# The first FFN's weights: split once, stored to DRAM, loaded in the second run

## The chip, the cores and the metric

The kernel runs on one core of a Trainium2 chip. The metric is the device time of one execution in microseconds; the time before is the median of three executions. The profile is of one further execution.

## The reference, cut to what matters

One layer of an encoder is applied with the same weights to two batches, a prompt of 1024 tokens and a sample of 256, each of width 1024. All is in fp32.

```
x <- LN1(alpha*x + 0.5*SwiGLU_1(x))
x <- LN2(alpha*x + W_out[RMS(S5(x)) ; RMS(Hyena(x))])
x <- LN3(alpha*x + 0.5*SwiGLU_2(x))

SwiGLU(x) = (silu(x @ w_gate) * (x @ w_up)) @ w_down     # w_gate, w_up (1024, 2816), w_down (2816, 1024)
```

The change touches the first line alone, `SwiGLU_1`. The second line has a state-space part (S5), whose matrices are made from small parameters, and long convolutions (Hyena), whose filters are made and transformed by the kernel.

## The kernel before, in words

TensorE reads its operands in a shorter fp32 format (`F32R`). To keep fp32's precision each operand is split in two parts: `hi`, its value rounded to that format, and `lo`, what the rounding left. A product is then three matmuls: hi x hi, hi x lo and lo x hi. The helper `split` (L171, L172) makes the parts: ScalarE copies the source into `hi`, VectorE subtracts `hi` from the source into `lo`.

The hidden width of 2816 is 22 tiles of 128 (`NFT`), called tiles of f. The first FFN runs twice over all its weights, since not all tokens fit in SBUF at once. `fa` (L1635) has four tiles of 128 tokens, two of the sample and two of the prompt, 512 tokens in all; `fb` (L1634) has the other six tiles of the prompt, 768 tokens, in chunks of 512 and 256. Both go through the function `ffn` (L254).

In `ffn`, a weight number i stands for one half of a tile of f: i = 2 ft is gate, i = 2 ft + 1 is up. `weights(i)` (L273) loads raw fp32 columns on SP's queue (L281) into one of two raw buffers (128 columns at a time in `fa`, 256 in `fb`) and splits 128 of them into one of two buffers `wgu`, each (128, 2, 8, 128): part, slice of the model width, column. `gate_up(ft)` (L287) calls `weights(i)` and, one ahead, `weights(i + 1)`, runs the matmuls of gate and of up (L298; per weight 24 matmuls for each chunk of tokens), and forms h = 0.5 * silu(gate) * up (L306, L307), which is split too. Down goes in groups of tiles of f: `size` is 2 by default, so nine groups of two and a last one of four. `wdown(ft)` (L316) splits a raw tile of w_down that `load_down` (L311, L314) loaded on SP's queue; `fa` has one raw buffer for these and `fb` two, and the next load is issued behind the split that frees the buffer. `down(grp, ...)` (L324) sums 3 matmuls for each tile of f of the group in one PSUM bank for each tile of tokens and half of the width (L331), and VectorE adds the bank into x (L336 for the first group, L338 for the others). Before a group's `down`, the gate and up of the next group's first tile are issued. In the last group each tile of tokens gets its layer norm and is stored to DRAM (L1601).

The work is woven: `weave` (L1644) interleaves the steps of `fa` with those of the filters (`filter_spectra`; its matmuls are on L695 to L774), and L1645 those of `fb` with the preparation of S5 (`s5_prep`, `s5_mats`: small matmuls on L611 to L628, many small VectorE operations, stores of matrices on L637 and of tables). The order of issue gives each instruction its priority, and a list scheduler, which goes by its own estimates, fixes from it the order of each engine's instructions. On the chip each engine works in that order; semaphores for every dependence are put in by the framework. DMAs of `nc.sync` are issued by SP, those of `nc.scalar` by ScalarE, those of `nc.gpsimd` by POOL. Before the change POOL issues no DMA of the program; it has the small `pow` of the layer norms (L230).

SBUF is cut in 25 pieces, which buffers take and give back. In the last group of `fb` the function `to_mix` (L1621) reloads two tiles of x1 (L1583), which `fa` had stored, and transposes them on TensorE (L221) ahead of the next stage, the in-projection (`mix_in`, L857).

## Time and profile before

| | |
|---|---|
| median of three executions | 2579.18 us (2578.24 to 2588.45) |
| the profiled execution | 2584.32 us, of which the span of the program's instructions is 2582.5 us |
| TensorE matmuls busy | 2523.1 us, 98% of the span |
| TensorE weight loads (PEld, beside the matmuls) | 2112.1 us, 82% |
| VectorE (DVE) busy | 1810.0 us, 70% |
| ScalarE (ACT) busy | 812.3 us, 31% |
| GpSimd (POOL) busy | 74.7 us, 3% |
| moved by DMA | 326.44 MB |

Busy time of TensorE is the union of its matmuls' spans, which overlap; how fast they follow each other has to be read from runs of many. `fa` and the filters take about the first 500 us, `fb` with the preparation of S5 goes on to about 1125 us. In the windows, "DMA share" is the mean busy share of the core's 16 DMA engines, and PEclk the granted share of TensorE's full clock.

### The profile page before, as it was taken

Reading aid. Unit: us, or ns where it says so; the run is one execution under the profiler, and the core shown is the slowest. Engines: PE = TensorE matmul, PEld = TensorE weight load, DVE = VectorE, ACT = ScalarE, POOL = GpSimd, SP = SyncE. Lnnn points to the kernel's source line nnn. Section 1 sums busy time; section 2 is a strip of 40 time slices with the busy share of each in tenths; the row PEclk is TensorE's granted clock in tenths of the full one; section 3 lists DMA queues with packets and bytes.
Section 4 is the critical chain, followed back from the end, with each engine's and each line's share of the span. In section 5 each row is a group of like instructions: output and inputs, shape, how many; then the busy total and the mean of one; then the engine's idle time right before and its main releaser. Section 6 shows DMA issues by size and latency. Waiting matters only on the chain.

```text
span 2582.5 us, 32676 instructions
## 1 busy us (share of the span) xinstructions
PE 2523.1 (98%) x12833; PEld 2112.1 (82%) x12833; DVE 1810.0 (70%) x3016; ACT 812.3 (31%) x1218; POOL 74.7 (3%) x58
## 2 busy tenths in 40 slices
PE   8999999999999999999999999999989999999998
PEld 6767887888888888788888878898768888888887
DVE  6777777568944666557896888788886556556437
ACT  5443344321322222223444313333332222223200
POOL 0000000000000000000000000000230000000001
PEclk9999999999999999999999999999999999999999
DMA  6332333533632333355566754564432223245311
GB/s 198 117 88 83 106 102 98 171 103 110 166 86 75 109 100 104 87 156 146 170 179 180 237 189 145 168 189 151 141 114 90 89 74 98 74 143 191 124 40 65
DMA packets 329073, 326.44 MB, mean 126 GB/s; under 512 B 41068, under 2 KB 285445, under 8 KB 328150
## 3 DMA queue, kind: packets, MB, share of 16 engines
q1 hardware_dynamic: 293366, 305.99, 37.5%
q10 hardware_dynamic: 35552, 18.36, 2.7%
q8 instruction: 101, 1.65, 0.3%
q14 instruction: 54, 0.44, 0.1%
HBM read 249.57 MB, written 74.46 MB: 125 GB/s over the span
## 4 chain that ended last, share of the span: by engine, by line
PE 82%; DVE 12%; DMA 3%; issue 2%; POOL 1%; ACT 1%; SPq 0%; DVEq 0%; ACTq 0%; POOLq 0%
PE banks L298 26%; PE banks L1367 16%; PE banks L331 12%; PE banks L1510 8%; PE banks L857 4%; PE banks L1238 3%; DVE s L927 3%; PE banks L774 3%; PE banks L1060 2%; DVE s L172 2%; PE banks L1201 1%; DVE s L245 1%; PE banks L1113 1%; DVE s L975 1%; DMA s<-in_ffn_w_gate_dram 1%
## 5 line engine op out<-in xcount | busy, mean ns | idle before, releaser
L298 PE MATMUL banks<-s,s 128*128 128x512 f32 (+1 forms) x4224 | 792.8, 342 | 3.3 <-ACT s L171 2.5
L298 PEld LDWEIGHTS banks<-s,s 128*128 128x128 f32 x4224 | 650.4, 190 | 99.6 <-issue 10.7
L171 ACT ACTIVATE s<-s 128x1024 fp32r<-128x1024 f32 (+3 forms) x467 | 437.8, 955 | 860.7 <-PE banks L298 239.0
L172 DVE TENSOR_TENSOR s<-s,s 128x1024 fp32r<-128x1024 f32 (+3 forms) x467 | 505.1, 1096 | 193.2 <-ACT s L171 191.0
L1367 PE MATMUL banks<-s,s 128*128 128x512 f32 x1848 | 423.4, 391 | 4.3 <-DVE s L172 3.4
L1367 PEld LDWEIGHTS banks<-s,s 128*128 128x128 f32 x1848 | 347.5, 188 | 78.7 <-DVE s L172 4.9
L331 PE MATMUL banks<-s,s 128*128 128x512 f32 x1584 | 393.0, 396 | 2.0 <-DVE s L172 1.0
L331 PEld LDWEIGHTS banks<-s,s 128*128 128x128 f32 x1584 | 291.2, 189 | 64.2 <-issue 2.1
L857 PE MATMUL banks<-s,s 128*128 128x512 f32 (+1 forms) x1152 | 238.1, 361 | 0.0
L1510 PE MATMUL banks<-s,s 128*128 128x512 f32 x704 | 216.8, 389 | 0.2 <-DVE s L172 0.2
L857 PEld LDWEIGHTS banks<-s,s 128*128 128x128 f32 x1152 | 188.3, 190 | 28.1 <-DVE s L172 0.4
L338 DVE TENSOR_TENSOR s<-banks,s 128x512 f32<-128x512 f32 x204 | 139.1, 688 | 49.1 <-PE banks L331 48.0
L1510 PEld LDWEIGHTS banks<-s,s 128*128 128x128 f32 x704 | 132.1, 188 | 28.1 <-DVE s L172 0.7
L1383 DVE TENSOR_TENSOR s<-banks,s 128x512 f32<-128x512 f32 x110 | 75.9, 690 | 106.5 <-PE banks L1367 105.7
L1510 PE MATMUL banks<-s 128*128 128x512 f32 x352 | 136.9, 389 | 0.0
L1238 PE MATMUL banks<-s,s 128*128 128x512 f32 x480 | 125.2, 409 | 3.2 <-ACT s L171 1.6
L1516 DVE TENSOR_TENSOR s<-banks,s 128x512 f32<-128x512 f32 x80 | 55.0, 690 | 97.1 <-PE banks L1510 97.1
L230 POOL TENSOR_TENSOR cst<-cst 128x1 f32<-128x1 f32 (+2 forms) x38 | 49.9, 1313 | 2496.0 <-DVE cst L229 2496.0
L1238 PEld LDWEIGHTS banks<-s,s 128*128 128x128 f32 x480 | 90.1, 192 | 23.1 <-ACT s L171 2.0
L307 DVE SCALAR_TENSOR_TENSOR s<-banks,s 128x512 f32<-128x512 f32 (+1 forms) x88 | 47.6, 554 | 84.3 <-PE banks L298 83.4
L543 DVE TENSOR_TENSOR s<-s,cst 128x288 f32<-128x288 f32 (+1 forms) x128 | 53.5, 438 | 53.5 <-PE banks L623 26.9
L676 DVE TENSOR_TENSOR s<-banks,s 128x512 f32<-128x512 f32 (+2 forms) x112 | 59.2, 552 | 44.4 <-ACT s L793 20.4
(210 smaller groups left out, 2347.8 us busy)
## 6 DMA issues: line engine op xcount, KB each, us to landing
s<-in_ffn_w_down_dram SPq DMA_DIRECT2D x88, 512.0 KB
s<-in_ffn_w_gate_dram SPq DMA_DIRECT2D x66, 512.0 KB
s<-in_ffn_w_up_dram SPq DMA_DIRECT2D x66, 512.0 KB
s<-in_ffn_w_gate_dram SPq DMA_DIRECT2D x11, 1024.0 KB
s<-in_ffn_w_up_dram SPq DMA_DIRECT2D x11, 1024.0 KB
scr_h<-s SPq DMA_DIRECT2D x22, 512.0 KB
s<-scr_h SPq DMA_DIRECT2D x22, 512.0 KB
scr_tab<-s ACTq DMA_DIRECT2D x64, 160.0 KB
```

The source lines that it names most:

```text
L171: K.nc.scalar.activation(out=hi, in_=src, func=AF.Copy)
L172: K.nc.vector.tensor_tensor(out=lo, in0=src, in1=hi.bitcast(F32), op=ALU.subtract)
L298: nc.tensor.matmul(pss[-1][c], lhsT=w[:, wv, d], rhs=xT.parts[k][c].at(d), start=(d == 0 and wv == 0 and k == 0), stop=(d == 7 and wv == 1))
L331: nc.tensor.matmul(ps, lhsT=h[s // 4][:, a, s % 4 * 128:(s % 4 + 1) * 128], rhs=w[:, b, dh * 512:(dh + 1) * 512], start=(n == 0), stop=(n ...
L338: nc.vector.tensor_tensor(out=xv, in0=ps, in1=xv, op=ALU.add)
L774: nc.tensor.matmul(ps, lhsT=F[kt][a].v[:, s, i], rhs=b.v[:, s], start=(n == 0), stop=(n == 3 * NT // R - 1))
L857: nc.tensor.matmul(p, lhsT=w[:, wv, d], rhs=xT[nm].parts[k][c].at(d), start=(d == 0 and wv == 0 and k == 0), stop=(d == 7 and wv == 1))
L927: TT = lambda o, a, b, op: V.tensor_tensor(out=o, in0=a, in1=b, op=op)
L1238: nc.tensor.matmul(ps, lhsT=y[s // per][a].v[:, k, ts], rhs=W[k].v[:, b, dh * 512:dh * 512 + 512], start=(k == 0 and a == 0 and b == 0), s ...
L1367: self.K.nc.tensor.matmul(ps, lhsT=w[i][:, d], rhs=x[k][:, d], start=first and m == 0, stop=m == len(todo) - 1, skip_group_check=True)
L1383: TT = lambda o, a, b: V.tensor_tensor(out=o, in0=a, in1=b, op=ALU.add)
L1510: nc.tensor.matmul(ps, lhsT=p[a].v[:, 1, o:o + 128], rhs=p[b].v[:, 0, dh * 512:dh * 512 + 512], start=m == 0, stop=m == len(todo) - 1)
```

## The change

`fa` gets a setting `keep`: after each split of a weight, SP stores both its parts to DRAM, as (128, 2, 8, 128) for each of 44 gate/up weights and as (128, 2, 1024) for each of 22 down weights, 1 MB (8 KB a partition) each. `fb` gets `parts`: it has no raw buffers and no splits of weights, and POOL loads the stored parts straight into the buffers that the matmuls read. `fb` also gets three `wgu` buffers in place of two, and `size` 3: six groups of three tiles of f and the last one of four, with three buffers for down's parts and four for h.

```diff
@@ -259,7 +259,8 @@
     unit, size = cfg.get("unit", 1), cfg.get("size", 2)
     chunks = chunks_of(T)
     fw = cfg.get("raw", 256)
-    raw = K.ring(2, 8, fw)
+    parts, keep = cfg.get("parts"), cfg.get("keep")
+    raw = None if parts else K.ring(2, 8, fw)
     wgu = K.ring(cfg.get("wgu", 2), 2, 8, 128, dt=F32R)
     bg = Banks(K, cfg["bg"])
     bd = Banks(K, cfg["bd"])
@@ -274,6 +275,10 @@
 
         ft, up = divmod(i, 2)
         if ft >= NFT or i in ready:
+            return
+        if parts:
+            ready[i] = w = wgu.get()
+            nc.gpsimd.dma_start(out=w, in_=parts[0][i])
             return
         o = ft * 128 % fw
         if o == 0:
@@ -283,6 +288,8 @@
         ready[i] = w = wgu.get()
         with K.tc.high_priority(offset=cfg.get("ahead", 0)):
             split(K, rawgu[up][:, :, o:o + 128], w[:, 0], w[:, 1])
+        if keep:
+            nc.sync.dma_start(out=keep[0][i], in_=w.bitcast(F32))
 
     def gate_up(ft):
         pss = []
@@ -297,7 +304,7 @@
             for d, wv, c, k in todo:
                 nc.tensor.matmul(pss[-1][c], lhsT=w[:, wv, d], rhs=xT.parts[k][c].at(d),
                                  start=(d == 0 and wv == 0 and k == 0), stop=(d == 7 and wv == 1))
-        if ft == NFT - 1:
+        if ft == NFT - 1 and raw:
             raw.free()
         hv = [h.get() for h in hr] if ft < NFT - 4 + size + 1 else [extra(2, n) for _, n in chunks]
         with K.tc.high_priority(offset=cfg.get("hp", 0)):
@@ -309,15 +316,20 @@
         return hv
 
     def load_down(ft):
-        if ft < NFT:
+        if ft < NFT and not parts:
             rawdn[ft] = rawd.get()
             nc.sync.dma_start(out=rawdn[ft], in_=wd[ft * 128:(ft + 1) * 128, :])
 
     def wdown(ft):
+        w = wdn.get() if ft < NFT - 4 + size else extra(2, D)
+        if parts:
+            nc.gpsimd.dma_start(out=w, in_=parts[1][ft])
+            return w
         r = rawdn.pop(ft)
-        w = wdn.get() if ft < NFT - 4 + size else extra(2, D)
         with K.tc.high_priority(offset=cfg.get("ahead", 0)):
             split(K, r, w[:, 0], w[:, 1])
+        if keep:
+            nc.sync.dma_start(out=keep[1][ft], in_=w.bitcast(F32))
         load_down(ft + len(rawd.bufs))
         return w
 
@@ -347,7 +359,7 @@
     groups = [tuple(range(f, min(f + size, NFT - 4))) for f in starts] + [tuple(range(NFT - 4, NFT))]
     weights(0)
     yield 0.01
-    rawd = K.ring(cfg.get("rawd", 1), D)
+    rawd = K.ring(0 if parts else cfg.get("rawd", 1), D)
     wdn = K.ring(size, 2, D, dt=F32R)
     hr = [K.ring(size + 1, 2, n, dt=F32R) for _, n in chunks]
     tmp = K.ring(2, chunks[0][1])
@@ -1554,7 +1566,7 @@
     g = lambda k: A[k][0]
     dp = ctx.enter_context(tc.tile_pool(name="dr", bufs=1, space=bass.MemoryType.DRAM))
     shapes = {"mat": (128, 32, 5, 128), "tab": (128, 16, 2, 2, 2, 160), "u": (512, 8, 160), "g": (512, 8, 160),
-              "rate": (2048,), "h": (NFT, 128, 1024), "x2": (128, 8, D)}
+              "rate": (2048,), "gu": (2 * NFT, 128, 2, 8, 128), "down": (NFT, 128, 2, D), "h": (NFT, 128, 1024), "x2": (128, 8, D)}
     for nm in NAMES:
         L, NT, R = PARTS[nm]
         shapes.update({"spec_" + nm: (2, 2, L // R // 128, 128, 2, R, 256), "x1_" + nm: (128, NT, D), 
@@ -1631,9 +1643,9 @@
 
 
 
-    fb = ffn1([("prompt", s) for s in range(2, 8)], dict(bg=(0, 1, 2, 3), bd=(4, 5), tail=to_mix, rawd=2), turn1)
+    fb = ffn1([("prompt", s) for s in range(2, 8)], dict(bg=(0, 1, 2, 3), bd=(4, 5), tail=to_mix, wgu=3, size=3, parts=(scr["gu"], scr["down"])), turn1)
     fa = ffn1([("sample", 0), ("sample", 1), ("prompt", 0), ("prompt", 1)],
-              dict(bg=(0, 1), bd=(2, 3), raw=128, tail=lambda: steps(fb, 1)))
+              dict(bg=(0, 1), bd=(2, 3), raw=128, tail=lambda: steps(fb, 1), keep=(scr["gu"], scr["down"])))
     steps(fa, 1)
     for nm, v in (("eye16", K.eye16), ("sgn", K.sgn)):
         nc.sync.dma_start(out=v, in_=A[nm])
```

## Rows read from the trace of the kernel before

**Rows 1.** The page's first part: each engine's busy time, share and instructions.
```profile
PE 2523.1 (98%) x12833; PEld 2112.1 (82%) x12833; DVE 1810.0 (70%) x3016; ACT 812.3 (31%) x1218; POOL 74.7 (3%) x58
```

**Rows 2.** The chain of waits, two unbroken runs: start us, us, what.
```profile
206.66 6.77 PE banks L774 x56
...
455.45 8.21 PE banks L331 x36
```

**Rows 3.** Windows of four stages: stretch, length, busy us (instructions), PEclk, DMA share, GB/s.
```profile
0.00:500.00 500.00, 482.96 (x2315) 381.34 (x2316) 356.12 (x511) 213.93 (x264) 0.20 (x4) 0.99 0.38 120
500.00:1050.00 550.00, 549.92 (x2988) 468.45 (x2987) 368.97 (x983) 141.54 (x269) 5.12 (x4) 1.00 0.36 106
1050.00:1125.00 75.00, 70.81 (x370) 59.44 (x369) 51.41 (x91) 14.02 (x26) 8.72 (x6) 0.98 0.46 133
1125.00:1570.00 445.00, 430.24 (x2295) 366.30 (x2293) 345.09 (x541) 166.16 (x305) 10.17 (x6) 1.00 0.58 177
```

**Rows 4.** TensorE's waits, 0 to 500, then 500 to 1125 us: total, times, longest.
```profile
PE banks L221 <- DMA s<-in_x_sample_dram: 5.6, 2, 5.0
PE banks L746 <- DVE s L742: 4.8, 6, 1.3
PE banks L695 <- DMA s<-in_feat_prompt_dram: 3.1, 1, 3.1
...
PE banks L298 <- ACT s L171: 0.9, 1, 0.9
...
PE banks L221 <- DMA s<-scr_x_prompt: 4.2, 1, 4.2
```

**Rows 5.** Groups by line and shape, 500 to 1075 us: busy us, mean ns | idle before.
```profile
L172 DVE TENSOR_TENSOR s<-s,s 128x1024 fp32r<-128x1024 f32 x67 | 81.3, 1219 | 44.7 <-ACT s L171 44.7
L338 DVE TENSOR_TENSOR s<-banks,s 128x512 f32<-128x512 f32 x104 | 71.3, 690 | 30.4 <-PE banks L331 29.8
L171 ACT ACTIVATE s<-s 128x1024 fp32r<-128x1024 f32 x67 | 70.0, 1059 | 217.3 <-PE banks L298 128.6 <-PE banks L331 71.3 <-issue 15.7
```

**Rows 6.** Windows around a 1 MB gate load, then two 512 KB down loads, in fb.
```profile
775.00:780.00 5.00, 5.00 (x30) 4.36 (x30) 0.05 (x1) 0.00 (x0) 0.00 (x0) 1.00 0.68 210
801.00:806.00 5.00, 5.00 (x30) 4.34 (x30) 1.11 (x1) 0.02 (x1) 0.00 (x0) 1.00 0.63 206
```

**Rows 7.** SP's timeline, 12 to 60 us: start, us, what.
```profile
14.27 0.37 SPq L281 DMA_DIRECT2D s<-in_ffn_w_gate_dram  x1
...
29.72 0.58 SPq L314 DMA_DIRECT2D s<-in_ffn_w_down_dram  x1
...
40.41 0.34 SPq L314 DMA_DIRECT2D s<-in_ffn_w_down_dram  x1
...
51.93 0.37 SPq L281 DMA_DIRECT2D s<-in_ffn_w_gate_dram  x1
```

**Rows 8.** Windows of fa's first part.
```profile
15.00:35.00 20.00, 20.00 (x83) 15.61 (x83) 13.48 (x32) 10.09 (x13) 0.00 (x0) 0.91 0.63 177
35.00:50.00 15.00, 15.00 (x64) 11.52 (x64) 13.25 (x18) 14.66 (x17) 0.00 (x0) 1.00 0.89 299
50.00:75.00 25.00, 24.66 (x116) 18.51 (x115) 20.91 (x36) 9.75 (x14) 0.00 (x0) 1.00 0.25 74
75.00:125.00 50.00, 49.74 (x230) 37.84 (x229) 38.18 (x60) 23.79 (x33) 0.00 (x0) 1.00 0.41 130
```

**Rows 9.** SP's timeline, 262 to 300 us, down's loads of one group.
```profile
271.28 0.34 SPq L314 DMA_DIRECT2D s<-in_ffn_w_down_dram  x1
...
279.32 0.33 SPq L314 DMA_DIRECT2D s<-in_ffn_w_down_dram  x1
```

**Rows 10.** ScalarE's waits, 0 to 500 us: total us, times, longest.
```profile
ACT s L171 <- DMA s<-in_ffn_w_down_dram: 8.0, 4, 3.5
```

**Rows 11.** The chain of waits at the end of fb: start us, us, what.
```profile
1081.31 2.45 DMA scr_mat<-s
...
1083.77 6.13 DMA s<-scr_x_prompt
```

## The prediction

> **What bounds the kernel now.** I read the page's totals first [rows 1]: TensorE is busy for 2523.1 of 2582.5 us, VectorE for 70% and ScalarE for 31%. A busy TensorE need not be a fast one, so I next asked what one matmul costs in an unbroken run. The chain of waits has such runs [rows 2]: 36 matmuls of 512 columns in 8.21 us are 228 ns each, 56 of 256 columns in 6.77 us are 121 ns each. One tile of f in the second run fb (768 tokens) is 48 matmuls of 512 columns and 48 of 256 for gate and up, and 36 of 512 for down: 48 x 0.228 + 48 x 0.121 + 36 x 0.228 = 25.0 us; times 22 tiles 549 us. The windows [rows 3] give fb's main stretch, 500 to 1050 us, as 550 us with TensorE idle for 0.08 us. So fb already goes at the pace of its columns; whatever ScalarE and VectorE do there is covered. In the first run fa, 0 to 500 us, TensorE is idle for 17.0 us, and its waits [rows 4] name the first loads of x, the filters' reductions and one load of features: the FFN's weights cost 0.9 us. In 1050 to 1125 us it is idle for 4.2 us, one wait, for rows of x1 reloaded at the end of fb.
>
> **The change part by part.** The sum is made against the profiled execution: a span of 2582.5 us in a run of 2584.3, 5.1 us above the median of 2579.2.
>
> Removed in fb: 44 splits of gate/up weights and 22 of down weights. Each is 1.059 us on ScalarE and 1.219 us on VectorE [rows 5]: 66 x 1.059 = 70 us and 66 x 1.219 = 80 us of 141.5 and 369.0 us busy [rows 3]. Down in threes makes 7 groups of f instead of 10, so 3 x 12 = 36 fewer additions out of PSUM at 0.690 us, 25 us of VectorE. TensorE's matmuls stay the same in number and size. It waits for none of the removed work, so these 105 us of VectorE are worth what TensorE idled: 0.08 us. I take 0, bounds 0 to -0.1.
>
> Added in fb: 66 loads of 1.05 MB through POOL's queue in place of 22 such loads and 22 of half the size on SP. Trace of before shows no load issued by POOL. The nearest row is a 1 MB load on SP [rows 6]: 0.68 of 5 us, 3.4 us of all 16 DMA engines, and its traffic ends inside these 5 us. With three buffers a gate/up load may start two weights ahead, 2 x (24 x 0.228 + 24 x 0.121) = 16.8 us before it is read; the three down loads wait for the previous group's down and have two to three gate_up (16.8 us each) ahead of them. What queues behind a waiting load on POOL is only the next load and, at the very end, the layer norm's small pow. Bounds: 0, and for loads slower than the nearest row see the rivals. I take 0. DMA share in fb: 0.36 x 550 = 198 us, less 22 x 3.4 and 22 x 1.6 (half of 3.15) [rows 6], plus 66 x 3.4, gives 312 of 550 us.
>
> The Trainium skill ("DMA: Bandwidth & Descriptors", Measured) puts a 1 MB load issued from GpSimd at 6.15 us; by it, as an estimate, 66 take 406 us of fb's 550 and would stay hidden too. No run here shows that figure.
>
> Added in fa: 66 stores of 1.05 MB on SP, each behind the split that makes it. At 3.4 us each, the load's price (the store of this size and shape is not in the trace; below, 0 if the engines took it beside the rest), they need 224 us of the 16 engines, where fa now uses 0.38 x 500 = 190 [rows 3]. Together 414 of 500: it fits on average, not everywhere. Four effects:
>
> (a) *The first 50 us.* Loads of x, of the filters' transforms and the fastest run of weights meet here. Up to 50 us seven gate/up splits and two of down are done (SP takes up each next load as a split ends; [rows 7] has the first and the last of the seven, and down's two), so 9 x 3.4 = 30.6 us of stores. Free between 15 and 50 us: 20 x 0.37 + 15 x 0.11 = 9.1 us [rows 8]. The excess, 21.5 us, sits in the same queue as the next raw weights, which TensorE needs every 24 x 0.228 = 5.5 us. Bounds 0 and +21.5. Two raw buffers and the filters' own matmuls take up part of it; I take +8, nearer the low end, since the wait for weights there is 0.9 us today.
>
> (b) *Down's single raw buffer.* A split frees it, and the store, queued first, now goes ahead of the next load: 3.4 us later per tile. Two such issues lie 8.04 us apart today [rows 9], and ScalarE waits 8.0 us in all on these loads in fa [rows 10]. Nine groups of two have one split so exposed and the last four have three, most of them with a gate_up of 10.9 us between them and the matmuls that read them. Bounds 0 and 12 x 3.4 = +41; I take +5, nearer the low end, where ScalarE's 8.0 us lie.
>
> (c) *The split's write into a buffer that the store still reads.* It must land before the weight after next: two weights are 10.9 us apart at the fastest, a load's traffic ends within 5 [rows 6]. Hidden; if the engines are full it is the same excess as in (a), not a second one.
>
> (d) *SP's time.* 66 issues of some 0.37 us [rows 7] are 24 us of 500. SP mostly waits for buffers. 0, at most +2 by a late filter load.
>
> *The end of fb.* The reload of x1 starts only after the last store of the S5 matrices has landed [rows 11]; TensorE idles 4.2 us. With 105 us of VectorE freed beside it, the S5 preparation should end sooner, and SP's small loads with it: -4. Against it: the last group's four down weights come by POOL, and one of them landing late is a wait of up to 5 us. Bounds -4.2 and +5.
>
> Sum: +8 +5 +0 +0 +0 -4 = +9 us; 2584.3 + 9 - 5.1 = 2588 us.
>
> **The rivals.**
>
> *B: the DMA engines fill up in fa* (slower). One mechanism: 9 stores against 9.1 us of free engine time before 50 us, and then 0.25 and 0.41 of it already in use up to 125 us [rows 8], so raw weights stay late and down's chain with them. It decides from the point where a raw load lands later than one weight's 5.5 us after its buffer is free. Price: 21.5 us, and a third of (b)'s bound, 14 us, less the 4 at the end: 2579.2 + 31.5 = 2611; with all of (b) 2638. For it: 0.89 and 0.63 of the engines are taken in that stretch. Against: the wait for weights now is 0.9 us, so there is slack not seen.
>
> *C: all stores hidden, only the end of fb moves:* 2579.2 - 4.2 = 2575. For it: the filters give TensorE other work after 50 us. Against: TensorE's order is fixed, and it does not go round a late weight.
>
> *D: POOL's loads come too slowly.* fb needs 3 x 1.05 MB per 25.0 us, 126 GB/s; the row has 210 GB/s over its 5 us. Were they held to 100 GB/s, 66 x 10.5 = 693 us would stand where 550 do: +143, 2722. Nothing in the trace shows a converting load, for or against. A second way there is that VectorE holds POOL up: even in the 550 - 369 + 105 = 286 us in which it then does nothing there would be 4.3 us per load. The Trainium skill ("SBUF — State Buffer", SBUF: two separate sides) says that GpSimd can't write descriptors while VectorE runs an instruction in a 2-port mode. No run here shows that.
>
> *E: the freed VectorE is worth more than the end of fb.* If the S5 preparation running ahead also removes the idle time of 1125 to 1570 us, 14.8 us [rows 3], it is 2579.2 - 4.2 - 14.8 = 2560. Against: that stage's input is made by its own matmuls.
>
> *The change doesn't do what it says:* none left; the splits of fb go whatever the order.
>
> **How the numbers follow.** About 0.5%, 12.9 us, is what a measurement of this kernel tells from no change: faster is under 2566, slower over 2592. Forecast (2579 to 2600) 0.42, of which 0.34 within and 0.08 slower; B 0.28, slower; C 0.20, of which 0.17 within and 0.03 faster; D 0.04, slower; E 0.06, of which 0.05 faster. Faster 0.08, same 0.52, slower 0.40. The range 2568 to 2620 leaves out most of E, the upper third of B and D: about 0.17.
>
> **What would show it.** Right: fb's stretch still about 550 us with TensorE idle for under 1 us, splits of 128x1024 down by 66, DMA share in fa near 0.8; new TensorE waits behind L171 or L172 between 25 and 80 us; the x1 wait at the end of fb shorter. Wrong: fa's part as long as before with a DMA share under 0.7 (C), TensorE waiting on POOL's loads (D), or fb's stretch shorter than 549 us, which would mean that its matmuls did not go at the pace of their columns.

## The result, and the profile after

The changed kernel takes 2626.39 us (median of 4 runs, 2621.42 to 2627.7), the kernel before 2579.02 us beside it: a ratio of 1.0172, 95% interval 1.0144 to 1.0199. That is 47 us slower, 38 us above the forecast and 6 us above the top of its range. The profiled execution has a span of 2625.7 us against 2582.5, so 43.2 us can be followed in the trace.

The page after: totals, and the loads issued by GpSimd (count, KB each, median us from issue to landing).

```profile
PE 2541.8 (97%) x12833; PEld 2122.3 (81%) x12833; DVE 1716.2 (65%) x2914; ACT 743.6 (28%) x1148; POOL 110.7 (4%) x124
...
s<-scr_gu POOLq DMA_DIRECT2D x44, 1024.0 KB, 5.4
...
s<-scr_down POOLq DMA_DIRECT2D x22, 1024.0 KB, 8.6
```

Against [rows 1] the work went as the change says: the same 12833 matmuls, 102 VectorE instructions fewer (66 splits, 36 additions) and 94 us less of VectorE, 69 us less of ScalarE. But TensorE, which sets the time, is busy 18.7 us longer with the same matmuls (2541.8 against 2523.1) and idle 24.5 us longer (the rest of the 43.2).

To see where, I cut both spans at two ends: the last gate/up matmul of the first run fa, and the last down matmul of the second run fb. Windows of the kernel before (stretch, length, busy us and count by engine, granted clock of TensorE, DMA share, GB/s):

```profile
0.00:500.50 500.50, 483.46 (x2318) 381.72 (x2319) 356.12 (x511) 213.93 (x264) 0.20 (x4) 0.99 0.38 120
500.50:1119.20 618.70, 614.43 (x3326) 522.82 (x3325) 415.07 (x1065) 155.56 (x294) 12.38 (x9) 1.00 0.37 107
1119.20:2582.50 1463.30, 1425.25 (x7192) 1207.54 (x7191) 1038.83 (x1442) 442.79 (x660) 62.06 (x45) 0.99 0.43 137
```

And of the changed kernel:

```profile
0.00:514.50 514.50, 491.45 (x2318) 385.01 (x2319) 352.13 (x509) 206.73 (x258) 1.47 (x6) 0.98 0.72 241
514.50:1160.20 645.70, 623.76 (x3333) 527.89 (x3332) 326.03 (x966) 93.92 (x230) 47.39 (x73) 0.98 0.52 165
1160.20:2625.70 1465.50, 1426.59 (x7186) 1209.45 (x7184) 1038.03 (x1440) 442.98 (x660) 61.84 (x45) 0.99 0.43 136
```

fa is 14.0 us longer: 6.0 idle and 8.0 busy. fb, here with the end of fa's down in it, is 27.0 us longer: 17.7 idle and 9.3 busy. The rest, 2.2. Part of the longer busy time is the granted clock, which falls to its lower level (1.2 in place of 2.4 GHz) behind the stalls. By the trace's clock records the lower level lasts 20.5 us in fa where it lasted 13.6, and 20.5 us in fb where it lasted 3.4; at half speed these differences are worth 3.4 and 8.5 us. So the clock adds about half of a stall's length. It makes nearly all of fb's 9.3 us, but not half of fa's 8.0; the other 4.6 us there I can't place.

The order of the instructions has changed too, which the prediction did not reckon with. The list scheduler goes by its own estimates, and with the stores in the program it puts fa's work in another order on TensorE, VectorE and ScalarE. TensorE's differs from the 81st matmul on; its timeline there, before and after (start, us, what):

```profile
28.24 0.64 PE L695 MATMUL banks<-s,cst 17*64 17x256 f32 x2
```

```profile
24.73 8.78 PE L305 MATMUL banks<-s,s 128*128 128x512 f32 x38
```

Before, two matmuls of the filters (L695) stand there between those of gate and up; after, 38 of gate and up (L305) go in a row. So fa's 14 us are the price of the stores together with this order. What each would cost alone no run separates.

TensorE's waits after, 0 to 515 us and then 514.5 to 1160.2 us (total us, times, longest):

```profile
PE banks L221 <- DMA s<-in_x_sample_dram: 5.8, 2, 5.3
PE banks L758 <- DVE s L754: 4.3, 9, 1.4
PE banks L343 <- ACT s L171: 3.7, 1, 3.7
...
PE banks L343 <- DVE s L350: 7.7, 3, 6.5
PE banks L623 <- DVE s L555: 5.3, 2, 3.8
PE banks L221 <- DMA s<-in_x_prompt_dram: 4.9, 2, 3.8
```

Beside [rows 4], three kinds are new. In fa, down (L343) waits for the split of its weights (L171). At the start of fb, the transposes (L221) wait for rows of x. And later in fb, down waits for its own additions (L350), and the S5 matrices' matmuls (L623) for VectorE. The wait for reloaded rows of x1 at fb's end, 4.2 us before, is gone.

**fa's first 50 us.** SyncE's timeline after, 12 to 60 us (start, us, what):

```profile
13.80 4.94 SPq L292 DMA_DIRECT2D scr_gu<-s  x2
18.79 0.43 SPq L286 DMA_DIRECT2D s<-in_ffn_w_gate_dram  x1
...
38.59 2.86 SPq L292 DMA_DIRECT2D scr_gu<-s  x2
...
43.13 0.90 SPq L321 DMA_DIRECT2D s<-in_ffn_w_down_dram  x1
...
45.65 1.91 SPq L286 DMA_DIRECT2D s<-in_ffn_w_gate_dram  x1
...
59.87 0.38 SPq L321 DMA_DIRECT2D s<-in_ffn_w_down_dram  x1
```

Down's raw loads here come at 43.13 and 59.87, where [rows 7] has loads of down at 29.72 and 40.41; a gate load that went out at 14.27 now stands behind two stores, at 18.79. TensorE stands for 3.7 us at 52 us, and from 50 to 100 us the clock is at 0.93. The windows of the first and the next 50 us, before and after:

```profile
0.00:50.00 50.00, 41.36 (x171) 31.63 (x172) 31.86 (x60) 30.45 (x37) 0.20 (x4) 0.97 0.75 229
50.00:100.00 50.00, 49.66 (x227) 37.22 (x225) 40.15 (x63) 23.87 (x32) 0.00 (x0) 1.00 0.38 117
```

```profile
0.00:50.00 50.00, 40.74 (x156) 30.46 (x157) 25.12 (x55) 22.09 (x29) 0.20 (x4) 0.97 0.82 263
50.00:100.00 50.00, 45.99 (x199) 34.95 (x198) 34.75 (x51) 22.07 (x28) 0.00 (x0) 0.93 0.75 266
```

**fa's end.** GpSimd's timeline (start, us, what, idle before), then the chain of waits, both of the changed kernel:

```profile
509.42 0.73 POOL L326 DMA_DIRECT2D s<-scr_down  x1 [508.97 <-DMA scr_down<-s]
512.13 0.54 POOL L281 DMA_DIRECT2D s<-scr_gu  x1 [1.99 <-PE banks L305]
514.85 1.06 POOL L281 DMA_DIRECT2D s<-scr_gu  x2 [2.18 <-PE banks L305]
515.89 1.08 POOL L326 DMA_DIRECT2D s<-scr_down  x2
```

```profile
508.64 6.17 DMA s<-in_ffn_w_down_dram
...
517.68 15.76 DMA s<-in_ffn_w_down_dram
...
533.47 1.06 ACT s L171
```

Six 1 MB loads for fb go out within 8 us. fa's last raw load of down, issued behind them, lands after 15.76 us, where the one before it took 6.17, and fa's down cannot end before it. In the kernel before, the same load, the last of fa's 22, went out 39 us earlier:

```profile
478.73 0.33 SPq L314 DMA_DIRECT2D s<-in_ffn_w_down_dram  x1
```

So the stores bring the load late, and fb's loads then slow it.

**Inside fb.** Two pieces of the chain of waits after, near 701 and 995 us:

```profile
697.31 7.68 DMA scr_tab<-s
...
706.95 0.61 DVE s L350
...
707.61 7.41 PE banks L343 x24
...
992.40 4.72 DMA scr_mat<-s
...
999.45 0.66 PE banks L623 x2
```

A store of the S5 preparation takes 7.68 us to land. VectorE works in order and stands on the buffer, down's additions (L350) wait behind it, both of down's banks are full, and TensorE loses 6.5 us. At 995 us VectorE stands on another store, and the matmuls of the S5 matrices (L623) wait for it.

### The profile page after: what moved, and what is told of

Read it like the earlier page. It is cut to its first block, busy times and chain, and to the rows that moved or that the text cites. A ratio compares the mean times of both kernels' runs of the same rounds, so it can differ in the third digit from the quotient of the medians.

```text
span 2625.7 us, 32641 instructions
## 1 busy us (share of the span) xinstructions
PE 2541.8 (97%) x12833; PEld 2122.3 (81%) x12833; DVE 1716.2 (65%) x2914; ACT 743.6 (28%) x1148; POOL 110.7 (4%) x124
## 4 chain that ended last, share of the span: by engine, by line
PE 76%; DVE 13%; DMA 6%; issue 2%; ACT 2%; POOL 1%; SPq 1%; ACTq 0%; DVEq 0%; POOLq 0%
PE banks L305 21%; PE banks L1379 16%; PE banks L343 12%; PE banks L1522 8%; PE banks L869 5%; PE banks L1250 3%; DVE s L939 3%; PE banks L786 3%; PE banks L1072 2%; DVE s L172 2%; DVE s L754 1%; PE banks L1213 1%; ACT s L171 1%; DMA s<-in_ffn_w_down_dram 1%; PE banks L1125 1%
## 5 line engine op out<-in xcount | busy, mean ns | idle before, releaser
L305 PE MATMUL banks<-s,s 128*128 128x512 f32 (+1 forms) x4224 | 796.4, 343 | 2.8 <-ACT s L171 2.2
L305 PEld LDWEIGHTS banks<-s,s 128*128 128x128 f32 x4224 | 653.6, 191 | 98.0 <-issue 7.5
L171 ACT ACTIVATE s<-s 128x1024 fp32r<-128x1024 f32 (+3 forms) x401 | 369.3, 938 | 713.8 <-DVE s L314 113.2
L172 DVE TENSOR_TENSOR s<-s,s 128x1024 fp32r<-128x1024 f32 (+3 forms) x401 | 425.5, 1076 | 179.8 <-ACT s L171 171.7
L343 PE MATMUL banks<-s,s 128*128 128x512 f32 x1584 | 400.1, 400 | 17.5 <-DVE s L350 9.5
L343 PEld LDWEIGHTS banks<-s,s 128*128 128x128 f32 x1584 | 294.1, 190 | 85.9 <-DVE s L350 12.9
L350 DVE TENSOR_TENSOR s<-banks,s 128x512 f32<-128x512 f32 x168 | 114.1, 686 | 58.2 <-PE banks L343 57.5
L1395 DVE TENSOR_TENSOR s<-banks,s 128x512 f32<-128x512 f32 x110 | 75.9, 690 | 106.2 <-PE banks L1379 105.4
L555 DVE TENSOR_TENSOR s<-s,cst 128x256 f32<-128x256 f32 (+1 forms) x128 | 54.3, 439 | 103.4 <-PE banks L635 65.0
L1528 DVE TENSOR_TENSOR s<-banks,s 128x512 f32<-128x512 f32 x80 | 55.0, 690 | 97.1 <-PE banks L1522 97.1
```

Source lines behind the costliest of these rows:

```text
L171: K.nc.scalar.activation(out=hi, in_=src, func=AF.Copy)
L172: K.nc.vector.tensor_tensor(out=lo, in0=src, in1=hi.bitcast(F32), op=ALU.subtract)
L305: nc.tensor.matmul(pss[-1][c], lhsT=w[:, wv, d], rhs=xT.parts[k][c].at(d), start=(d == 0 and wv == 0 and k == 0), stop=(d == 7 and wv == 1))
L343: nc.tensor.matmul(ps, lhsT=h[s // 4][:, a, s % 4 * 128:(s % 4 + 1) * 128], rhs=w[:, b, dh * 512:(dh + 1) * 512], start=(n == 0), stop=(n ...
L350: nc.vector.tensor_tensor(out=xv, in0=ps, in1=xv, op=ALU.add)
L1395: TT = lambda o, a, b: V.tensor_tensor(out=o, in0=a, in1=b, op=ALU.add)
```

## The experiments

For each kernel I read four stretches off its profiled execution: fa up to its last gate/up matmul; from there to fa's last down matmul (fa's end; fb's start lies inside it, with 4 matmuls of fb's gate in the kernel before, 11 in the changed one, one in sp_loads and none in loads_only, 0.228 us each); from there to fb's last down matmul; the rest. Spans, us; the median and the ratio to the kernel before are those of the timed runs.

```
kernel          fa     fa's end  fb     rest    span    median   ratio (95%)
before          500.5  28.4      590.3  1463.3  2582.5
after           514.5  40.8      604.9  1465.5  2625.7  2626.39  1.0172 (1.0144-1.0199)
stores_only     513.6  30.6      589.7  1466.0  2599.9  2599.00  1.0068 (1.0052-1.0085)
loads_only      496.7  27.5      598.1  1465.0  2587.3  2592.58  1.0051 (1.0034-1.0067)
stores_small    503.7  28.4      588.1  1462.9  2583.1  2587.06  1.0025 (1.0014-1.0036)
size2           516.6  39.4      606.8  1465.6  2628.4  2628.41  1.0180 (1.0162-1.0198)
tab3            516.9  40.8      607.1  1462.6  2627.4  2629.79  1.0190 (1.0173-1.0207)
sp_loads        516.0  30.1      597.5  1461.8  2605.4  2605.68  1.0092 (1.0076-1.0109)
down_sp         517.1  37.7      599.9  1459.6  2614.3  2616.68  1.0137 (1.0122-1.0152)
act_stores      535.6  46.6      602.5  1462.4  2647.1  2648.31  1.0251 (1.0233-1.0270)
pool_stores     547.3  27.5      606.6  1462.5  2643.9  2643.96  1.0248 (1.0230-1.0266)
pool_st_sp_ld   552.4  27.5      590.2  1464.3  2634.4  2628.84  1.0180 (1.0155-1.0205)
loads_once      515.2  40.2      585.0  1459.5  2599.9  2604.71  1.0104 (1.0076-1.0131)
paced           516.5  42.1      612.1  1466.6  2637.3  2639.59  1.0233 (1.0215-1.0251)
st_late         501.0  30.5      589.8  1465.1  2586.4  2592.17  1.0043 (1.0028-1.0058)
st_no_down      513.1  27.5      591.8  1462.7  2595.1  2594.69  1.0049 (1.0032-1.0066)
late_sp         502.8  30.2      591.1  1465.9  2590.0  2591.90  1.0047 (1.0030-1.0064)
```

What one profiled execution can tell is seen where the instructions are the same. Eight kernels have the same fa, in the same order on TensorE (after, stores_only, size2, tab3, sp_loads, down_sp, loads_once, paced); it takes 513.6 to 517.1 us. loads_only has the fa of the kernel before, in the same order, and fb's first load goes out only at 491.6; yet it is 3.8 us shorter. The rest of the kernel, which the change leaves alone, takes 1459.5 to 1466.6 us. So a difference of some 4 us in one stretch shows nothing by itself. The profiled execution of the kernel before (2584.3 us) is also 5.3 us above its median, so that spans against it look some 5 us too good.

Where an edit touched the stores, the scheduler also ordered fa anew. stores_small, st_late, late_sp, st_no_down and act_stores each have an order of fa that is neither that of before nor that of after; pool_stores and pool_st_sp_ld keep nearly that of before (TensorE's first difference is at the 173rd matmul, at 58 us). Where fa of these is compared with another kernel's, the order is part of the difference. In fb the loads' experiments (loads_only, sp_loads, down_sp, pool_stores, loads_once, late_sp) are ordered nearly as in after, while size2 and paced are not.

### One part of the change alone

**stores_only**: the stores, with fb as before.

```
- dict(..., wgu=3, size=3, parts=(scr["gu"], scr["down"]))
+ dict(..., rawd=2)
```

> The first run stores both parts, the second run works as in the kernel before (its own raw loads and splits), so the stored parts are read by nobody. Theory 1 (the stores' traffic in fa): fa's gate and up end some 14 us late as in the changed kernel, and part of the 12 us at fa's end comes too, so 2579 + 14 to 26 = 2593 to 2605. Rival (the loss comes from fb, where VectorE is freed and POOL loads): at most 2585. If all 47 us come from the stores: 2626.

Measured 2599.0, as theory 1 has it: the stores alone, with the order that they bring, cost 17 us of span (medians, 19), 13.1 of it in fa.

**loads_only**: no stores; fb loads the same number of bytes from the weights' own memory.

```
- ..., keep=(scr["gu"], scr["down"])))
+ ...))
- parts=(scr["gu"], scr["down"])
+ parts=(srcs + srcs, downs + downs)
...   # srcs: pieces of 1 MB of w_gate and w_up, downs: of w_down
```

> The second run loads both parts with POOL and takes down three tiles at a time as in the changed kernel, but the first run stores nothing; the loads read 66 MB of the same shape from the weights' own memory, so fb's numbers are not those of the layer. Theory 1: fa as before, fb keeps its own loss of some 15 us: 2594; the last raw loads of fa still queue behind POOL's first loads, up to +5. Rival (all of the loss is the stores' traffic): 2575 to 2580. If fb's loss needs the stores' late end: under 2585.

Measured 2592.6, as theory 1 has it, but without the loss at fa's end: the loads alone cost 13 us by the medians. fa's end stays at 27.5 us, since without stores fa's last raw load of down goes out at 475.24, ahead of fb's first at 491.60. So the 40.8 of the changed kernel needs stores and loads together. The two parts, 19 and 13, leave some 14 of the 47.

**stores_small**: as stores_only, with 64 KB in each store.

```
- nc.sync.dma_start(out=keep[0][i], in_=w.bitcast(F32))
+ nc.sync.dma_start(out=keep[0][i][:, 0, 0], in_=w.bitcast(F32)[:, 0, 0])
- nc.sync.dma_start(out=keep[1][ft], in_=w.bitcast(F32))
+ nc.sync.dma_start(out=keep[1][ft][:, 0, 0:128], in_=w.bitcast(F32)[:, 0, 0:128])
```

> As the kernel that only stores, but each store takes 64 KB (one sixteenth) of its buffer: the same 66 issues on SP, the same waits for the split and for the buffer, a sixteenth of the traffic. Theory 1 (traffic): 2577 to 2584. Rival (SP's order and the waits, not the traffic): within 4 us of the kernel with full stores, 2593 or more.

Measured 2587.1, between the theory and its rival, fa 503.7: with a sixteenth of the bytes the stores cost 7.5 us by the medians, where full ones cost 19.4. So some 12 of the 19 come with the bytes; how much of that is traffic, and how much the other order of fa that the scheduler gives to smaller stores, is not separated. fa's 3.2 us are less than one profile can tell.

**size2**: the changed kernel with down in twos.

```
- wgu=3, size=3, parts=
+ wgu=3, size=2, parts=
```

> The changed kernel with down in groups of two again in fb, all else as changed. Theory 1: groups of three cost and give nothing to TensorE: 2622 to 2630. Rival (nine matmuls a bank, or three 1 MB loads at a time on POOL, delay fb): 2605 to 2615, as fb's 15 us would go.

Measured 2628.4 against 2626.4, with intervals that overlap: the groups of three are worth nothing measurable.

### fa: which stores cost

**st_late**: as stores_only, without its first nine stores (there six of them go out before 50 us and the last at 61).

```
- if keep:
+ if keep and i >= 7:      # gate, up
- if keep:
+ if keep and ft >= 2:     # down
```

> The first run stores, the second run is as before the change, and the stores of the first seven gate and up tiles and the first two down tiles are left out (9 of 66; nothing reads what is stored). With all 66 it was 2599.0 us, the first run's gate and up ending at 513.6 us against 500.5. If the prediction's term (a) is right, the excess of the first 50 us made 8 us: 2590 to 2592 us, the first run ending at 505 to 506. If the cost goes with the bytes: 9/66 of 19.5 us, 2.7 less, 2596 us, ending near 512. If the stalls at 52 and 100 us stay as they are: no gain, 2598 to 2600.

Measured 2592.2, fa 501.0, 12.6 us less than in stores_only. The medians give 6.8 us, and they are the better measure: the profiled execution of st_late has the lowest time of its four (2588.5 us), that of stores_only the highest of its four (2601.6). So 9 of 66 stores carry 7 to 13 us, with the order that goes with them: TensorE's order in st_late is that of before up to its 348th matmul, at 88 us, and that of stores_only differs from the 81st on. SyncE's timeline of st_late, 12 to 60 us, has down's loads back at their places of [rows 7]:

```profile
13.79 0.37 SPq L286 DMA_DIRECT2D s<-in_ffn_w_gate_dram  x1
...
29.30 0.58 SPq L321 DMA_DIRECT2D s<-in_ffn_w_down_dram  x1
...
40.00 0.34 SPq L321 DMA_DIRECT2D s<-in_ffn_w_down_dram  x1
```

From 200 to 500 us its DMA share is 0.70, as with all the stores (0.68 in stores_only), yet fa ends within 0.5 us of the kernel before: there it costs nothing that a profile can tell.

**st_no_down**: as stores_only, without down's 22 stores.

```
-        if keep:
-            nc.sync.dma_start(out=keep[1][ft], in_=w.bitcast(F32))
```

> The first run stores gate and up only (44 of 66 stores), the second run is as before the change. If the prediction's term (b) is right, down's raw buffer, freed later for its next load, made 5 us: 2593 to 2595 us. If that chain made all of it, as the stall at 52 us on ScalarE's split for down suggests: 2584 to 2588 us, the first run ending at 501 to 504. If the cost goes with the bytes, a third of 19.5 us: 2592 to 2593, ending near 509.

Measured 2594.7: 4 us less than stores_only, with intervals that overlap, and fa is as long (513.1). fa's end is 3.1 us shorter, but fb is 2.1 us longer; 0.9 us of this is four matmuls of fb's gate (0.228 us each), which lie on the other side of the cut here. So the 4 us can't be placed. Of the theories, "all of it" is out; (b)'s 5 us fit the time but are not shown. The stall at 52 us is gone, and in its place stands the one for the load of features, 3.9 us (3.1 before [rows 4], 0.8 in stores_only), with 10.2 us at the lower clock behind it.

**act_stores**: the changed kernel's stores issued by ScalarE.

```
- nc.sync.dma_start(out=keep[0][i], ...)     + nc.scalar.dma_start(out=keep[0][i], ...)
- nc.sync.dma_start(out=keep[1][ft], ...)    + nc.scalar.dma_start(out=keep[1][ft], ...)
```

> The changed kernel with the 66 stores issued by ScalarE in place of SyncE. Theory: the stores cost by their traffic (64 KB stores with the same waits cost a third), so another queue changes little: 2624 to 2629 us. Rival: the store stands ahead of the next raw load on SyncE and its wait for the split holds that load back; then the first run ends 3 to 6 us earlier, 2620 to 2623 us. Against both: a store on ScalarE waits for VectorE's half of the split and holds ScalarE's next split behind it: 2632 us and more.

Measured 2648.3, 22 us worse than the change: fa 535.6, its end 46.6. The time is that of the third expectation; whether by its mechanism I have not taken apart.

**pool_stores**: the same on GpSimd, which has next to nothing to do in fa.

```
- nc.sync.dma_start(out=keep[0][i], ...)     + nc.gpsimd.dma_start(out=keep[0][i], ...)
- nc.sync.dma_start(out=keep[1][ft], ...)    + nc.gpsimd.dma_start(out=keep[1][ft], ...)
```

> The changed kernel with the 66 stores issued by GpSimd, which is all but idle in the first run, in place of SyncE. Theory of traffic: the first run's gate and up end stays at 514 us (500 before), the whole at 2624 to 2629 us, since the same bytes go through the same 16 engines. Rival: a store on SyncE stands ahead of the next raw load, with its wait for the split and with 1 MB in the same queue; on a queue of its own it no longer does, the first run ends 5 to 10 us earlier and the whole is at 2615 to 2621 us. Against both: the loads of the second run stand behind the last stores in GpSimd's queue and come late: over 2630 us.

Measured 2644.0, fa 547.3, against the theory and its rival. The time is in the third expectation's range, but the loss lies in fa and not in late loads of fb (fa's end is 27.5). Off SyncE's queue the stores do more harm: 46.8 us in fa against the kernel before, with nearly its order. The chain of waits of pool_stores at its longest stall shows how:

```profile
142.13 8.84 DMA scr_spec_sample<-s
...
150.99 8.37 DMA s<-in_feat_prompt_dram
...
159.40 1.11 PE banks L707
```

A store of the filters, and the load of features behind it, take 8.84 and 8.37 us (5.06 and 5.27 before, 3.02 and 6.27 in the changed kernel); TensorE waits 10.0 us, where it waited 3.1 for this load before [rows 4]. In act_stores it is 8.6 us for the same load. With the stores in SyncE's own queue, in the changed kernel, it is 0.4 us. I read it so: SyncE's order was not the stores' cost but their restraint, since there a store stands behind the loads that were issued before it, and on a queue of its own it moves beside them. This is argued and not shown: the changed kernel also has another order of fa.

### fb: which loads cost

**sp_loads**: the changed kernel with fb's loads on SyncE.

```
- nc.gpsimd.dma_start(out=w, in_=parts[0][i])
+ nc.sync.dma_start(out=w.bitcast(F32), in_=parts[0][i])
- nc.gpsimd.dma_start(out=w, in_=parts[1][ft])
+ nc.sync.dma_start(out=w.bitcast(F32), in_=parts[1][ft])
```

> The changed kernel with the second run's loads of the stored parts issued by SyncE, so that they stand in the same queue behind the first run's last raw loads. Theory of the collision at the first run's end: the last raw down load (15.76 us from issue to landing) is no longer beside six 1 MB loads of another queue; the two stalls of TensorE at 520 and 532 us (4.0 and 2.1 us) and the half clock behind them (3.4) go: about 2617 us. Rival: SyncE takes its instructions in order, a load that waits for a ring buffer holds the S5 stores behind it and these hold VectorE; the gain at the first run's end is lost again, 2626 to 2640 us.

Measured 2605.7, 11 us better than the theory: 21 us of the 47 come back by the queue alone, 10.7 at fa's end (2.3 of them ten matmuls of fb's gate that lie behind the cut here) and 7.4 in fb. Whether it is SyncE's order or that GpSimd no longer issues them, this run does not separate. SyncE's timeline and the chain of waits of sp_loads around fa's last raw load:

```profile
518.28 0.35 SPq L321 DMA_DIRECT2D s<-in_ffn_w_down_dram  x1
518.74 1.94 SPq L281 DMA_DIRECT2D s<-scr_gu  x2
```

```profile
524.57 1.55 ACT s L171 x2
```

The load stands ahead of fb's loads now, and the split that needs it starts at 524.57, 6.3 us after its issue, not 15.8. The rival's blocked stores do not show as a loss: GpSimd's wait for TensorE's banks has become SyncE's, and the stall at 995 us is all but gone (L623 waits 1.2 us in place of 5.3).

**down_sp**: only down's loads on SyncE.

```
- nc.gpsimd.dma_start(out=w, in_=parts[1][ft])
+ nc.sync.dma_start(out=w.bitcast(F32), in_=parts[1][ft])
```

> The changed kernel with only the second run's down loads on SyncE; gate and up stay on GpSimd. Collision at the first run's end: three of the six loads that lie beside the last raw down load go behind it, so the stalls at 520 and 532 us should halve at least: 2618 to 2623 us. If these stalls come from the first run's stores and the x loads alone, nothing changes there: 2626 us. If SyncE's order costs more than it gives: over 2630 us.

Measured 2616.7: half way in the time, a little better than expected, but not at fa's end, which is 37.7: 3.1 of sp_loads' 10.7 us there. fa's last raw load takes 13.27 us with three of the six loads ahead of it and two behind. The rest of the gain is 5.0 us in fb and 5.9 us behind it, where the kernels are the same and which is scatter.

**pool_st_sp_ld**: the queues swapped, stores on GpSimd and loads on SyncE (the two diffs above).

> The changed kernel with the stores on GpSimd and the second run's loads on SyncE: the queues are swapped. With the loads on SyncE alone it was 2605.7 us. If SyncE's order makes part of the stores' cost: 2594 to 2601 us. If traffic makes all of it: 2603 to 2608 us.

Measured 2628.8, outside both expectations, since fa is as bad as in pool_stores (552.4); with the loads on SyncE fb takes 590.2 us, as before the change. It fits both readings, each in its own stretch; the profiled execution has the highest time of its four, 7.4 us above the median.

**loads_once**: the changed kernel in which fb keeps its first tiles.

```
- nc.gpsimd.dma_start(out=w, in_=parts[0][i])
+ if i < 3:
+     nc.gpsimd.dma_start(out=w, in_=parts[0][i])
- nc.gpsimd.dma_start(out=w, in_=parts[1][ft])
+ if ft < 3 or ft == NFT - 1:
+     nc.gpsimd.dma_start(out=w, in_=parts[1][ft])
```

> The changed kernel in which the second run loads only the first three gate and up tiles and four down tiles and uses them for all f; the rest of the loads is left out, and so the first FFN of the prompt's tiles 2 to 7 is computed with those weights. VectorE and ScalarE are freed as in the change, but the second run has almost no DMA traffic. Theory of traffic: the stalls at 701 and 995 us go, those at 520 to 536 us stay in part (six loads still stand there); the second run lasts 620 to 630 us in place of 645.7, the whole 2600 to 2612 us. Rival, VectorE's order: without the splits that paced it, VectorE runs through the S5 work in long stretches ahead of down's additions whatever the loads do; the stalls stay and the whole is at 2618 to 2627 us.

Measured 2604.7, as the theory of traffic has it, fb 585.0 in place of 604.9, fa's end unchanged at 40.2, where the first six loads still are. TensorE's waits of loads_once, 515.2 to 1140.4 us (its down is L345):

```profile
PE banks L221 <- DMA s<-in_x_prompt_dram: 4.8, 2, 3.7
PE banks L345 <- ACT s L171: 1.7, 1, 1.7
...
PE banks L625 <- DVE s L557: 0.6, 1, 0.6
```

The waits for L350 are gone with the traffic and those for VectorE in the S5 matrices (L555, here L557) are down to 0.6 us, though VectorE is as free as in the change. Without traffic fb is 5.3 us shorter than before.

**paced**: the work taken from ScalarE and VectorE is put back as a split that nothing reads (compare with size2).

```
- dict(..., wgu=3, size=3, parts=...)
+ dict(..., wgu=2, size=2, parts=...)
  nc.gpsimd.dma_start(out=w, in_=parts[0][i])
+ split(K, w[:, 0].bitcast(F32), trash.v, trash.v)
  nc.gpsimd.dma_start(out=w, in_=parts[1][ft])
+ split(K, w[:, 0].bitcast(F32)..., trash.v, trash.v)
```

> The changed kernel with groups of two and two gate and up buffers, in which each loaded tile is followed by a split of it into a tile that nothing reads: ScalarE and VectorE do the work that the change removed, the loads stay. Without that extra work the kernel with groups of two took 2628.4 us. Theory of VectorE's order: the S5 work is spread out again as before the change, the stalls near 710, 947, 1010 and 1073 us go (3.6, 3.5 and 3.4 us and the half clock behind them) and it is 10 to 16 us faster, 2612 to 2618 us, although VectorE and ScalarE have more to do. Theory of traffic: no gain, 2626 to 2632 us. Against both: the loads now sit ahead of a split with two buffers and come late, over 2635 us.

Measured 2639.6, 11 us slower than size2. Stalls stay (TensorE waits 10.2 us for VectorE in the S5 matrices, in 4 waits), so the extra splits do not take them away. It differs from size2 in its buffers and in the order of fb too, so neither are the 11 us the price of the splits alone, nor is the theory of VectorE's order ruled out by it.

**tab3**: a third buffer for the table tiles whose store VectorE stood on at 701 us.

```
- K.ring(2, 4, 160), K.ring(2, 4, 160), K.ring(1, 4, 160)
+ K.ring(3, 4, 160), K.ring(3, 4, 160), K.ring(1, 4, 160)
```

> The changed kernel with three buffers in place of two in the rings of the S5 table's cosine and sine tiles. Theory: the stall at 701 us is a buffer of that ring whose store to DRAM took 7.68 us under a DMA share of 0.88; VectorE stands on it 3.4 us in order, down's additions queue behind it, TensorE loses 6.55 us and then runs 6.8 us at the half clock, worth 3.4. A third buffer takes that away: 2616 to 2619 us, with the stall at 995 us still there. Rival: the table is only where VectorE's backlog shows this time; the idle comes back at another table or matrix tile: 2623 to 2628 us.

Measured 2629.8: the rival. The chain of waits of tab3 there:

```profile
693.38 5.74 DMA scr_tab<-s
699.32 0.29 DVE s L435
...
711.17 0.68 DVE s L350
711.89 3.35 PE banks L343 x7
```

VectorE's wait for a store of the table, from 690 to 715 us, in the changed kernel and in tab3 (total us, times, longest):

```profile
DVE s L436 <- DMA scr_tab<-s: 3.4, 1, 3.4
```

```profile
DVE s L436 <- DMA scr_tab<-s: 0.6, 1, 0.6
```

So the third buffer did take most of that wait away. But VectorE then has some 12 us of work in order, most of it on the table, and down's addition comes after it: TensorE waits 7.4 us instead of 6.5. The stall at 701 us is not the price of that one late store; VectorE's order has a share in it.

### Together

**late_sp**: fb's loads on SyncE, and the first nine stores left out.

```
- if keep:                                   + if keep and i >= 7:
- if keep:                                   + if keep and ft >= 2:
- in_=parts[0][i])                           + in_=parts[0][i if i >= 7 else i + 7])
- in_=parts[1][ft])                          + in_=parts[1][ft if ft >= 2 else ft + 2])
```

> The changed kernel with the second run's loads on SyncE and without the nine stores of the first 50 us; in place of the nine tiles that are not stored the second run loads nine others, so the bytes loaded are the same and the first FFN of the prompt's tiles 2 to 7 is computed with wrong weights in these places. If the causes add up: 2605.7 less 7 (by the medians of st_late) to 13 (by its spans), 2593 to 2599 us, the first run's gate and up ending near 502 and the second run lasting 625 to 629 us. Rival: the second run loses its place against VectorE and the S5 work once it begins 12 us earlier, and gives the gain back: 2602 to 2608 us. Either would be slower than before the change.

Measured 2591.9, ratio 1.0047 (1.003 to 1.0064), just under the expected range: 34 of the 47 us are gone and fb is at 591.1 us. What is left, 12 us by the medians and 7.5 by the spans, is spread over all four stretches and I have not taken it apart. No form of the change here is faster than the kernel before.

## Why the prediction was wrong

The forecast was 9 us slower than before, within what a measurement can't tell from no change; it is 47. Step by step:

- *What bounds the kernel.* Right. Freeing 89 us of VectorE and 62 us of ScalarE in fb (the windows' 415.07 to 326.03 and 155.56 to 93.92) gave nothing by itself; with the loads gone too, fb is 5.3 us shorter, about the wait at fb's end.
- *(a), the first 50 us, +8.* Near enough in size: 6.8 us by the medians, 12.6 by the stretches, inside its bounds of 0 to 21.5. The delay is as described: down's raw loads went out 13 to 19 us late and the 3.7 us wait for the split came. Two things the sum had left out: the clock fell behind the stalls (3.4 us in fa), and the scheduler ordered fa anew. How much of the 7 to 13 us is traffic and how much order is open. The store's price of 3.4 us of all engines was too high: the shares give 2.7, (0.72 x 514.5 - 0.38 x 500.5) / 66.
- *(b), down's single raw buffer, +5.* 4 us by the medians of st_no_down, within their noise, and not along fa. What the traces show of it is at fa's end: the last raw load of down goes out 39 us later, and that sets up the collision there.
- *(c) and (d), 0.* Stores of 64 KB cost 7.5 us by the medians (ratio 1.0025, 1.0014 to 1.0036), so the waits, SyncE's time and the new order are not free together. At 43 to 46 us, with the DMA share of the first 50 us at 0.82, SyncE's issues take 0.9 to 1.9 us, not 0.37.
- *fb's loads, 0.* This is the step that failed most. One load is as quick as I took it (a median of 5.4 us to landing, 8.6 for down's), and rival D did not come. The 6.15 us of the Trainium skill ("DMA: Bandwidth & Descriptors", Measured) lies between these two, though the page counts the time that the engines are busy, and the trace the time from issue to landing. But I compared 312 us of traffic with 550 us of stage, an average. The loads meet the S5 stores where these come in bursts, VectorE stands on a late store or has its work bunched behind it, and TensorE stands on VectorE: it is idle for 14.9 of the table's 604.9 us of fb, where I had said under 1. loads_once puts the loads of fb at 19.9 us, sp_loads at 7.4 for the queue's part.
- *No step for where the runs meet.* Six loads of fb, fa's last stores and raw load, and three loads of x stand within 8 us. That made 12.4 us of fa's end, some 1.6 of which are seven more matmuls of fb's gate that lie in that stretch. I had considered each run's traffic against its own work, and asked of GpSimd only whether its loads come in time for fb, not what they delay. loads_only (27.5) and stores_only (30.6) show that it takes both.
- *The end of fb, -4.* The wait is gone in the changed kernel, as forecast, and its 4.2 us are lost among the new stalls; loads_once has 5.3 us, which one profile can't tell from 4.

Rival B came nearest: full DMA engines in fa, at the price of 2611. In part that is luck: it put 35.5 us in fa, which cost 14.0 and 12.4 more at its end, and it has neither the second half of the kernel nor the clock. The share that I worked out for fa, 0.83 on average, was 0.72; from 200 us on 0.68 of the engines cost nothing that a profile can tell, and the first nine stores, which go out by 61 us, cost 7 to 13 us, though the share of the first 50 us was 0.75 before and 0.82 after. So the share alone does not tell the cost; what stands behind the transfer does.

What stays open: how fb's cost divides between slower transfers and the order in which VectorE meets them (tab3 and paced moved the stalls without a rule that I could name); how fa's divides between the stores' traffic and the order that the scheduler gave it, which a kernel with SyncE's stores and the order of before would tell; and whether GpSimd's queue costs more for its order or for who issues. Medians and spans differ by 7 to 8 us for loads_only, st_late and loads_once, because their profiled executions have the lowest time of their runs, 2.9 to 3.7 us under the median, and that of the kernel before lay 5.3 us above its own.

## What to carry to other kernels

Traffic that is added beside work that hides it is priced at the fullest 50 us and at the seams between stages, not by the stage's average: here the first 9 of 66 stores made 7 of the stores' 19 us. Try a transfer that nothing waits for behind the urgent ones in the same queue before giving it one of its own (here loads on SyncE gave 21 us back, stores on GpSimd cost 18 more). Where a scheduler orders the instructions, compare their order before and after: a new transfer can change it. And engine time freed off the critical path is worth only what TensorE waits for it, so read that wait before making room for it.

## What the runs showed of the hardware that was not expected

- With 1 MB stores on GpSimd's queue a store and a load of SyncE's took 8.84 and 8.37 us (pool_stores), where they took 5.06 and 5.27 before; with the stores on SyncE's own queue, and another order of fa, 3.02 and 6.27.
- An issue on SyncE grew from 0.34 to 0.58 us [rows 7] to 0.9 to 1.9 us at 43 to 46 us, with the DMA share of 0 to 50 us at 0.82.
- Stalls came with the lower clock behind them: fb has 17.7 us more idle time and 17.1 us more at the lower level, worth 8.5 us.
